# Score products of all attentions: the key's low part in a tile per head, 128 rows in both passes

## The chip, the cores and the metric

The kernel runs on one core of one Trainium2 chip. The metric is device time in microseconds (us), the median of several executions of the same program.

## What is computed

The reference is a network of four layers over 512 tokens and 1024 features, in float32. What matters here are its attentions: three kinds in the first two layers (a retention, a selected attention behind an indexer, a dilated attention), one in the third.

```
def hybrid_layer(x, ...):                    # twice
    proj = rms_norm(x, attn_norm_w) @ w_in
    ...                                      # retention 4 heads, selected attention 4, dilated 8, 64 features each
    x = x + mixed @ w_out
    return x + square(relu(rms_norm(x) @ w_up)) @ w_down
...
    logits = einsum('bqhd,bsd->bqhs', qib, k_idx)          # indexer: 8 query heads, one key
    inner = einsum('bhncd,bhnmd->bhncm', qc, kc) * decay   # retention
    s = einsum('bqhd,bshd->bhqs', qb, k) * scale           # the other attentions, then softmax, then @ v
```

Block 2 follows with an attention of 8 heads with forget gates (the "even" mixer), a gated linear recurrence (the "odd" mixer), and a gated feed-forward after each.

## The kernel before

Activations lie feature-major, [128 features, 512 tokens] per tile. A float32 operand is split into two float32r parts, high and low (`split`), and a product of two operands takes three passes on TensorE: high by high, high by low, low by high (`mm3`, lines 319 to 321). Weights are loaded by SyncE's queue, ScalarE makes the high part (line 266), VectorE or GpSimd the low part (line 267, tiles `whi`, `wlo`).

A score product (keys against queries of one head) has only 64 features to contract over, half of the 128 rows of the array. `head_product` (lines 305 and 306) makes it in two passes. In the first, one operand (`stacked`) has the high part of the head on 64 partitions and its low part on the other 64, and the other operand (`doubled`) has the high part twice, so that 128 rows give high by high and low by high at once. In the second pass, the 64 partitions of the high part meet the low part of the other operand: both operands are cut to `own`, the head's 64 partitions. `doubled` makes the low parts of a pair of heads as one tile `lo`, head 0 on partitions 0 to 63 and head 1 on 64 to 127 (line 297, on VectorE or GpSimd). The phase keeps two such tiles.

There are 208 score products: in each of the first two layers 24 of the indexer, 16 of the retention, 32 of the dilated attention and 16 of the selected one; in the third layer 32. `attend` issues the four products of a head (widths 128, 256, 384, 512), VectorE reduces each (line 521), ScalarE takes the exponential, VectorE and GpSimd scale (line 528), TensorE transposes (line 539), and `weighted_values` multiplies by the values (lines 488 and 490; the second with 64 columns of weights). Between heads, `fill()` lets other projections follow. The indexer's key exists once for all heads, already on all 128 partitions in two copies, high and low.

Each engine works through its own instructions in order. Their order comes from a scheduler that places each instruction by its own estimate when the program is built; a tile's buffer that is used again makes the new writer wait for the old readers. A background job on VectorE (`top_keys`, lines 643 and 644) takes the largest 128 scores step by step between the products.

Before the first weights arrive, `keep_warm(14)` issues 14 products on a zero bfloat16 tile that nothing reads.

Of the kernel before, what the change touches and what calls it, by code (L numbers as in the profile page):

```python
# [8 lines left out]
F = mybir.dt.float32  # L9
R = mybir.dt.float32r  # L10
# [5 lines left out]
S = 512  # L16
# [144 lines left out]
class Net:  # L161
    def __init__(self, ctx, tc, I, out):
# [22 lines left out]
        self.keep_warm(14)  # L185
# [28 lines left out]
    @contextmanager  # L214
    def phase(self, **bufs):
        """The tiles of one phase; the next phase's take their place."""
        with self.tc.tile_pool(name=self.name("phase"), bufs=1, reuse_waits="tile") as pool:
            self.pool, self.bufs = pool, bufs
            yield
# [4 lines left out]
    def act(self):  # L224
        """The two parts of a [128, 512] operand."""
        t = self.get("act", 2 * S, R)
        return t[:, :S], t[:, S:]
# [49 lines left out]
    def stacked(self, t, low=None):  # L277
        """The two parts of each of the two heads of t, one above the other: [high | low] of the first head and
        [low | high] of the second along the partitions."""
# [8 lines left out]
    def doubled(self, t, low=None):  # L288
        """The operand to go with stacked(): the high part of each of the two heads of t, twice along the
        partitions, and the low parts."""  # L290
        nc = self.nc
        ab, lo = self.act(), self.get("lo", S, R)
        for h, s in enumerate(ab):
            own, other = slice(64 * h, 64 * h + 64), slice(64 - 64 * h, 128 - 64 * h)
            nc.scalar.activation(s[own], t[own], AF.Copy)
            nc.scalar.activation(s[other], t[own], AF.Copy)
            (low or nc.vector).tensor_sub(lo[own], t[own], s[own].bitcast(F))
        return ab, lo

    def head_product(self, ps, hh, stacked, rows, doubled, cols, last=True):  # L300
        """ps = a.T @ b for head hh, a and b given by stacked() and doubled()."""
        mm = self.nc.tensor.matmul
        own = slice(64 * hh, 64 * hh + 64)
        a, (b, lo) = stacked[hh], doubled
        mm(ps, a[:, rows], b[hh][:, cols], start=True, stop=False, skip_group_check=True)  # L305
        self.last_mm = mm(ps, a[own, rows], lo[own, cols], start=False, stop=last, skip_group_check=True)  # L306

    def split_scaled(self, x, g, to=None):
        """x * g (per partition) into two parts."""
# [6 lines left out]
    def mm3(self, ps, w, a, first, last):  # L316
        """ps += w.T @ a for operands (high, low)."""
# [5 lines left out]
    def fm_tile(self, w, acts, off=0):  # L323
        """One 128-feature tile: [128 features, 512 tokens]."""
        return self.fm_tiles([(w, off)], acts)[0]

    def fm_tiles(self, ws, acts):
        """Several 128-feature tiles, all of them taking each chunk of acts as it comes, until the last two."""
# [14 lines left out]
    def catch_up(self):  # L343
        """What was put off until after some products."""
# [4 lines left out]
    def tm_half(self, ps, h, src, acts, width, low=None):  # L349
        """Half of the contraction of a token-major product; ps: a [128 tokens, width] psum for each block of  # L350
        128 tokens, made by the first half."""
# [16 lines left out]
    def tick(self):  # L368
        """Lets one step of the work in the background follow."""
# [3 lines left out]
    def after(self, inst, other):  # L373
        """Keeps inst from being issued ahead of other."""
# [3 lines left out]
    def not_before(self, inst):  # L378
        """Keeps work of the background from being issued ahead of the products it is to run beside."""
# [9 lines left out]
    def sumsq(self, chunks, g=None, acc=None, apart=False, eng=None):  # L389
        """The sum over chunks of their squares, each scaled by g(c) per partition; the last one apart, where  # L390
        the time to add it would show."""
# [15 lines left out]
    def mean_sq(self, accs, dim, eps=EPS, warm=False):  # L407
        """accs: [128, tokens] tiles, summed over partitions and tiles; the mean per token plus eps, token-major
        [128, 4]."""
# [13 lines left out]
    def keep_warm(self, n, after=None):  # L423
        """Products that nothing reads, for the tensor engine's clock to stay up while it waits."""
        ps = self.st_tile()
        for _ in range(n):
            mm = self.nc.tensor.matmul(ps, self.identb, self.identb.unsqueeze(1).to_broadcast([128, 4, 128]),
# [9 lines left out]
    def spread_psum(self, r):  # L437
        """r ([128 tokens, 4]) along the free axis, the same on all partitions: by three bfloat16 parts, which
        together are r."""
# [15 lines left out]
    def spread(self, r):  # L455
        """As spread_psum, in SBUF and after the products that follow first."""
# [9 lines left out]
    def values(self, n):  # L466
        """n tiles for the values of four heads, token-major, each head as [high | low]."""
# [5 lines left out]
    def put_values(self, v, tb, ps, r):  # L473
        """ps ([128 tokens, 4 heads x 64]) scaled by r [128,1] and split."""
# [6 lines left out]
    def weighted_values(self, o, hh, pt, v):  # L481
        """The rows of o for head hh: its values.T @ pt, over the causal blocks. The product of both parts of the
        values with the high part of pt takes one pass, low by high coming out below high by high."""
# [12 lines left out]
    def attend(self, pairs, fill):  # L496
        """Softmax attention of pairs of heads. Each of pairs gives, when its turn comes, q (already times
        -1/8) and k (feature-major), the values, mask(qb), added to the negated scores, an operand pair for
        a further term of these (or None) and what to do with the result [2 heads x 64, 512].
        fill() lets other products follow, for the tensor engine to do meanwhile."""  # L500
# [472 lines left out]
    def even_mixer(self):  # L973
# [41 lines left out]
        v = va  # L1015
# [271 lines left out]
```

## Time and profile before

| | |
|---|---|
| runs | 2552.95, 2553.09, 2555.98 us; median 2553.09 |
| profiled execution | span 2550.8 us from the first to the last instruction; the median lies 2.3 us above |
| TensorE matmul | 2482.1 us busy, 97% of the span, 11217 instructions |
| VectorE | 1361.0 us, 53% |
| ScalarE | 1042.9 us, 41% |
| GpSimd | 596.9 us, 23% |
| granted TensorE clock | 0.985 of full speed on average |

Matmul records overlap, since the ends of pipelined matmuls are modelled: the time that one takes from the next is read from start to start, not from its duration. The shares are averages over stages that have different limits. L305 is line 305 of the kernel before.

### The profile page before, as it was taken

Reading aid. Unit: us, or ns where it says so; the run is one execution under the profiler, and the core shown is the slowest. Engines: PE = TensorE matmul, PEld = TensorE weight load, DVE = VectorE, ACT = ScalarE, POOL = GpSimd, SP = SyncE. Lnnn points to the kernel's source line nnn. Section 1 sums busy time; section 2 is a strip of 40 time slices with the busy share of each in tenths; the row PEclk is TensorE's granted clock in tenths of the full one; section 3 lists DMA queues with packets and bytes.
Section 4 is the critical chain, followed back from the end, with each engine's and each line's share of the span. In section 5 each row is a group of like instructions: output and inputs, shape, how many; then the busy total and the mean of one; then the engine's idle time right before and its main releaser. Section 6 shows DMA issues by size and latency. Waiting matters only on the chain.

```text
span 2550.8 us, 28988 instructions
## 1 busy us (share of the span) xinstructions
PE 2482.1 (97%) x11217; PEld 1968.7 (77%) x11217; DVE 1361.0 (53%) x2216; ACT 1042.9 (41%) x1625; POOL 596.9 (23%) x395
## 2 busy tenths in 40 slices
PE   9999999999998999999999999999999989999997
PEld 6687788888876877888888777788887767788886
DVE  6968653333468686433336857533335865533434
ACT  5556552332355665422333464322223564322222
POOL 2355410110033643200111342110101453110101
PEclk9999999999998999999999999999999999999998
DMA  4311123222222111322222211222222222222221
GB/s 144 108 59 46 58 91 99 92 97 94 92 85 89 55 45 62 106 93 95 95 92 86 75 59 50 91 93 97 91 93 81 75 83 75 91 93 97 91 93 64
DMA packets 61514, 215.30 MB, mean 84 GB/s; under 512 B 6849, under 2 KB 6977, under 8 KB 61377
## 3 DMA queue, kind: packets, MB, share of 16 engines
q1 hardware_dynamic: 59760, 207.06, 24.6%
q0 software_dynamic: 1472, 6.29, 0.8%
q8 instruction: 88, 1.44, 0.2%
q14 instruction: 50, 0.40, 0.1%
q10 hardware_dynamic: 144, 0.11, 0.0%
HBM read 211.33 MB, written 2.10 MB: 84 GB/s over the span
## 4 chain that ended last, share of the span: by engine, by line
PE 85%; DVE 10%; issue 2%; ACT 2%; POOL 1%; DMA 0%; SPq 0%; DVEq 0%; ACTq 0%; POOLq 0%
PE mm L321 25%; PE mm L320 25%; PE mm L319 25%; PE st L306 3%; PE st L305 2%; DVE x L943 1%; PE st L539 1%; PE av L488 1%; PE av L490 1%; ACT xg L312 1%; PE av L414 1%; DVE hs L1169 1%; DVE xg L313 1%; DVE score L644 1%; DVE act L285 1%
## 5 line engine op out<-in xcount | busy, mean ns | idle before, releaser
L266 ACT ACTIVATE whi<-raw 128x1024 fp32r<-128x1024 f32 (+3 forms) x398 | 409.8, 1032 | 1156.8 <-PE mm L320 967.2
L319 PE MATMUL mm<-xg,whi 128*128 128x512 f32 x1792 | 704.0, 397 | 14.3 <-ACT xg L312 12.3
L321 PE MATMUL mm<-xg,wlo 128*128 128x512 f32 x1792 | 715.1, 399 | 2.1 <-DVE wlo L267 2.1
L320 PE MATMUL mm<-xg,whi 128*128 128x512 f32 x1792 | 714.2, 399 | 0.2
L319 PE MATMUL mm<-act,whi 128*128 128x512 f32 x1160 | 456.2, 396 | 10.2 <-ACT act L273 8.3
L321 PE MATMUL mm<-act,wlo 128*128 128x512 f32 x1160 | 461.9, 398 | 0.0
L320 PE MATMUL mm<-act,whi 128*128 128x512 f32 x1160 | 460.4, 397 | 1.4 <-POOL act L274 1.4
L267 DVE TENSOR_TENSOR wlo<-raw,whi 128x1024 fp32r<-128x1024 f32 (+2 forms) x289 | 348.5, 1207 | 136.3 <-ACT whi L266 135.5
L319 PEld LDWEIGHTS mm<-xg,whi 128*128 128x128 f32 x1792 | 340.9, 191 | 103.8 <-ACT xg L312 20.8
L274 POOL TENSOR_TENSOR act<-t,act 128x512 fp32r<-128x512 f32 x108 | 150.4, 1394 | 1106.0 <-ACT act L273 1073.3
L320 PEld LDWEIGHTS mm<-xg,whi 128*128 128x128 f32 x1792 | 338.4, 189 | 84.7 <-DVE xg L313 6.6
L321 PEld LDWEIGHTS mm<-xg,wlo 128*128 128x128 f32 x1792 | 338.0, 189 | 79.4 <-DVE wlo L267 4.5
L267 POOL TENSOR_TENSOR wlo<-raw,whi 128x1024 fp32r<-128x1024 f32 (+3 forms) x109 | 257.2, 2362 | 335.9 <-ACT whi L266 312.9
L319 PEld LDWEIGHTS mm<-act,whi 128*128 128x128 f32 x1160 | 221.4, 191 | 62.5 <-ACT act L273 9.7
L320 PEld LDWEIGHTS mm<-act,whi 128*128 128x128 f32 x1160 | 218.8, 189 | 53.7 <-POOL act L274 2.3
L321 PEld LDWEIGHTS mm<-act,wlo 128*128 128x128 f32 x1160 | 218.6, 188 | 47.5
L871 DVE TENSOR_TENSOR x<-x,mm 128x512 f32<-128x512 f32 x64 | 44.0, 688 | 206.2 <-PE mm L321 206.2
L863 DVE SCALAR_TENSOR_TENSOR t<-mm,rb 128x512 f32<-128x512 f32 x64 | 44.1, 691 | 198.8 <-PE mm L321 198.6
L1234 DVE TENSOR_TENSOR t<-mm,rb 128x512 f32<-128x512 f32 x44 | 30.4, 691 | 141.5 <-PE mm L321 141.5
L1232 DVE TENSOR_TENSOR t<-mm,rb 128x512 f32<-128x512 f32 x44 | 30.4, 691 | 118.1 <-PE mm L321 118.1
L273 ACT ACTIVATE act<-t 128x512 fp32r<-128x512 f32 x114 | 72.2, 633 | 49.2 <-DVE t L1235 32.9
L305 PE MATMUL st<-act,act 128*128 128x128 f32 (+3 forms) x208 | 77.5, 373 | 12.5 <-DVE act L285 7.8
(222 smaller groups left out, 2650.4 us busy)
## 6 DMA issues: line engine op xcount, KB each, us to landing
raw<-in_w1up SPq DMA_DIRECT2D x64, 512.0 KB, 3.3
raw<-in_w1down SPq DMA_DIRECT2D x64, 512.0 KB, 3.3
raw<-in_gate SPq DMA_DIRECT2D x44, 512.0 KB, 3.3
raw<-in_up SPq DMA_DIRECT2D x44, 512.0 KB, 3.3
raw<-in_w1fm SPq DMA_DIRECT2D x41, 512.0 KB, 3.3
raw<-in_down SPq DMA_DIRECT2D x32, 512.0 KB, 3.3
raw<-in_odin SPq DMA_DIRECT2D x16, 512.0 KB, 3.3
raw<-in_w1out SPq DMA_DIRECT2D x16, 384.0 KB, 3.0
```

Of the source, the lines that this page charges most:

```text
L266: nc.scalar.activation(hi[:, sl], raw[:, sl], AF.Copy)
L267: (low or nc.gpsimd).tensor_sub(lo[:, sl], raw[:, sl], hi[:, sl].bitcast(F))
L273: nc.scalar.activation(hi, t, AF.Copy)
L274: (low or nc.vector).tensor_sub(lo, t, hi.bitcast(F))
L305: mm(ps, a[:, rows], b[hh][:, cols], start=True, stop=False, skip_group_check=True)
L306: self.last_mm = mm(ps, a[own, rows], lo[own, cols], start=False, stop=last, skip_group_check=True)
L319: mm(ps, w[0], a[0], start=first, stop=False, skip_group_check=True)
L320: mm(ps, w[0], a[1], start=False, stop=False, skip_group_check=True)
L321: self.last_mm = mm(ps, w[1], a[0], start=False, stop=last, skip_group_check=True)
L863: nc.vector.scalar_tensor_tensor(t, ps, 0.0, rb, op0=OP.max, op1=OP.mult)
L871: nc.vector.tensor_add(x[j], x[j], ps)
L1232: nc.vector.tensor_mul(t, pg, rb)
```

## The change

`doubled` now makes a `lo` tile per head. GpSimd sets the other head's 64 partitions to zero, and the subtraction writes the own ones. `head_product` drops the cut to `own`: its second pass takes all 128 rows of the first pass's stationary operand and all 128 of `lo`, with zeros where the low part of the stationary operand stands. The phases keep four `lo` tiles in place of two, so a buffer still comes back after two pairs. For the indexer nothing is written to memory in addition: its low part already lies on all partitions, and its second pass now multiplies low by low as well. The first 14 products that keep the clock up take a zero float32r tile in place of the bfloat16 one, and the memory for descriptors of GpSimd's own transfers is set to 8192. Comments are gone too, and lines move by 1 to 3.

```
+        zero = self.cp.tile([128, 128], R, name="zero")
+        nc.vector.memset(zero.bitcast(F), 0.0)
-        self.keep_warm(14)
+        self.keep_warm(14, of=zero)
...
     def doubled(self, t, low=None):
-        ab, lo = self.act(), self.get("lo", S, R)
+        ab, lo = self.act(), [self.get("lo", S, R) for _ in range(2)]
         for h, s in enumerate(ab):
             own, other = slice(64 * h, 64 * h + 64), slice(64 - 64 * h, 128 - 64 * h)
+            nc.gpsimd.memset(lo[h][other].bitcast(F), 0.0)
             nc.scalar.activation(s[own], t[own], AF.Copy)
             nc.scalar.activation(s[other], t[own], AF.Copy)
-            (low or nc.vector).tensor_sub(lo[own], t[own], s[own].bitcast(F))
+            (low or nc.vector).tensor_sub(lo[h][own], t[own], s[own].bitcast(F))
         return ab, lo
 
     def head_product(self, ps, hh, stacked, rows, doubled, cols, last=True):
         mm = self.nc.tensor.matmul
-        own = slice(64 * hh, 64 * hh + 64)
         a, (b, lo) = stacked[hh], doubled
         mm(ps, a[:, rows], b[hh][:, cols], start=True, stop=False, skip_group_check=True)
-        self.last_mm = mm(ps, a[own, rows], lo[own, cols], start=False, stop=last, skip_group_check=True)
+        self.last_mm = mm(ps, a[:, rows], lo[hh][:, cols], start=False, stop=last, skip_group_check=True)
...
-        with self.phase(act=10, lo=2, v=2, o=1, pr=2, ph=2, pl=2, score=1, gt=2):
+        with self.phase(act=10, lo=4, v=2, o=1, pr=2, ph=2, pl=2, score=1, gt=2):
...
-                    self.head_product(ps[:, :n], hh, q, qs, ((ki[0], ki[0]), ki[1]), slice(0, n))
+                    self.head_product(ps[:, :n], hh, q, qs, ((ki[0], ki[0]), (ki[1], ki[1])), slice(0, n))
...
-        with self.phase(act=6, lo=2, v=2, o=1, pr=2, ph=2, pl=2, m=8, sg=1, row=2):
+        with self.phase(act=6, lo=4, v=2, o=1, pr=2, ph=2, pl=2, m=8, sg=1, row=2):
...
-    nc = _bacc.Bacc("TRN2", target_bir_lowering=False, num_devices=1)
+    nc = _bacc.Bacc("TRN2", target_bir_lowering=False, num_devices=1, dynamic_dma_scratch_size=8192)
```

TensorE's order stays as it was, line for line, but for the last heads of the first two layers, where the scheduler mixes passes of two heads and a projection a little differently. GpSimd's order gets 40 new instructions, 16 in each of the first two layers and 8 in the third. In the dilated attention of the first layer, GpSimd's instructions were these (`wlo` are low parts of weights, `pr` the softmax rows of a head that are being scaled, `act` a stacked operand):

```order
46 L267 TENSOR_TENSOR wlo_1864<-raw_1861,whi_1863 128x1024
47 L528 TENSOR_SCALAR pr_1647<-pr_1647,rc_1650 128x128
48 L528 TENSOR_SCALAR pr_1647<-pr_1647,rc_1650 128x256
49 L267 TENSOR_TENSOR wlo_1935<-raw_1932,whi_1934 128x1024
50 L267 TENSOR_TENSOR wlo_2023<-raw_2020,whi_2022 128x1024
```

At the same place the order is now this:

```order
58 L269 TENSOR_TENSOR wlo_1878<-raw_1875,whi_1877 128x1024
59 L297 MEMSET lo_2080 64x512
60 L531 TENSOR_SCALAR pr_1661<-pr_1661,rc_1664 128x128
61 L531 TENSOR_SCALAR pr_1661<-pr_1661,rc_1664 128x256
62 L269 TENSOR_TENSOR wlo_1952<-raw_1949,whi_1951 128x1024
63 L269 TENSOR_TENSOR wlo_2040<-raw_2037,whi_2039 128x1024
```

A MEMSET of the last dilated pair's low tile has come between the low part of weights and the scaling of a head's rows; it waits for the last score product of the third dilated head (head 0 of the second pair), whose tile had that buffer.

At the start of the second layer GpSimd's order was this (`act` belongs to the feed-forward before, `rstd` to the norm of the new layer):

```order
120 L274 TENSOR_TENSOR act_5151<-t_5148,act_5151 128x512
121 L434 TENSOR_TENSOR rstd_5468<-var_5466,mhalf 128x4
122 L267 TENSOR_TENSOR wlo_5669<-raw_5666,whi_5668 128x1056
```

Now it is this:

```order
140 L276 TENSOR_TENSOR act_5177<-t_5174,act_5177 128x512
141 L297 MEMSET lo_6082 64x512
142 L297 MEMSET lo_6083 64x512
143 L297 MEMSET lo_6221 64x512
144 L297 MEMSET lo_6222 64x512
145 L437 TENSOR_TENSOR rstd_5494<-var_5492,mhalf 128x4
146 L269 TENSOR_TENSOR wlo_5695<-raw_5692,whi_5694 128x1056
```

Four MEMSETs, which wait for tiles of the feed-forward in the same memory to come free, now stand ahead of the norm's `rstd`.

## Rows read from the trace of the kernel before

**Rows 1.** The page: busy time, share of the span and instructions of each engine.

```profile
PE 2482.1 (97%) x11217; PEld 1968.7 (77%) x11217; DVE 1361.0 (53%) x2216; ACT 1042.9 (41%) x1625; POOL 596.9 (23%) x395
```

**Rows 2.** The chain that ended last, shares of the span by line.

```profile
by line: PE mm L321 25.4%; PE mm L320 25.4%; PE mm L319 25.2%; PE st L306 2.7%; issue 2.0%; PE st L305 1.9%; DVE x L943 1.3%; PE st L539 1.0%; PE av L488 0.9%; PE av L490 0.8%; ACT xg L312 0.7%; PE av L414 0.6%; DVE hs L1169 0.6%; DVE xg L3
```

**Rows 3.** Instructions of line 306, forms kept apart; durations in ns, rows*columns of the array.

```profile
L306 PE MATMUL st<-lo,act x160: 322/435/792, 93.7 to 1545.1; 64*128 64x512 f32 x40, 64*128 64x384 f32 x40, 64*128 64x128 f32 x40, 64*128 64x256 f32 x40
```

**Rows 4.** Timeline of all engines around 60 us: start us, us, engine, line.

```profile
59.13 0.39 PE L319 MATMUL mm<-xg,whi 128*128 128x512 f32 x1
59.13 0.19 PEld L320 LDWEIGHTS mm<-xg,whi 128*128 128x128 f32 x1
...
60.02 0.69 DVE L587 TENSOR_TENSOR t<-mm,rb 128x512 f32<-128x512 f32 x1 [2.04 <-PE mm L321]
60.02 0.18 PEld L306 LDWEIGHTS st<-act,act 64*128 64x128 f32 x1 [0.24 <-issue]
60.02 0.38 PE L306 MATMUL st<-act,act 64*128 64x256 f32 x1
...
60.34 0.44 PE L305 MATMUL st<-act,act 128*128 128x384 f32 x1
```

**Rows 5.** Timeline of TensorE's matmuls, one dilated head and the values' products behind it.

```profile
179.52 0.22 PE L305 MATMUL st<-act,act 128*128 128x128 f32 x1
...
181.72 0.49 PE L306 MATMUL st<-lo,act 64*128 64x512 f32 x1
182.15 0.50 PE L488 MATMUL av<-ph,v 128*128 128x512 f32 x1
182.48 0.39 PE L490 MATMUL av<-pl,v 128*64 128x512 f32 x1
182.71 0.34 PE L488 MATMUL av<-ph,v 128*128 128x384 f32 x1
182.89 0.34 PE L490 MATMUL av<-pl,v 128*64 128x384 f32 x1
183.06 0.28 PE L488 MATMUL av<-ph,v 128*128 128x256 f32 x1
...
183.30 0.22 PE L488 MATMUL av<-ph,v 128*128 128x128 f32 x1
183.36 0.23 PE L490 MATMUL av<-pl,v 128*64 128x128 f32 x1
```

**Rows 6.** Windows: length, busy us of PE, PEld, DVE, ACT, POOL; clock; DMA.

```profile
60.00:80.00 20.00, 20.00 (x73) 13.12 (x73) 19.36 (x37) 11.25 (x21) 9.45 (x7) 1.00 0.32 104
80.00:100.00 20.00, 17.87 (x64) 13.14 (x63) 19.75 (x37) 15.03 (x22) 8.63 (x5) 0.86 0.26 91
200.00:220.00 20.00, 20.00 (x92) 15.60 (x92) 16.71 (x46) 12.17 (x24) 15.24 (x12) 1.00 0.19 60
240.00:260.00 20.00, 17.61 (x87) 13.15 (x85) 16.57 (x32) 16.11 (x34) 6.04 (x5) 1.00 0.12 35
1480.00:1500.00 20.00, 20.00 (x93) 15.31 (x94) 9.33 (x24) 9.71 (x20) 8.09 (x5) 1.00 0.20 63
```

**Rows 7.** Timeline of TensorE: two indexer products, and the retention's first product.

```profile
40.00 0.38 PE L306 MATMUL st<-act,act 64*128 64x256 f32 x1
...
55.36 0.49 PE L306 MATMUL st<-act,act 64*128 64x512 f32 x1
...
93.26 0.51 PE L305 MATMUL st<-act,act 128*128 128x512 f32 x1 [2.13 <-DVE act L285]
```

**Rows 8.** Timeline of GpSimd: a low part of weights, and its one large MEMSET.

```profile
180.96 2.38 POOL L267 TENSOR_TENSOR wlo<-raw,whi 128x1024 fp32r<-128x1024 f32 x1 [1.91 <-issue]
...
1386.22 0.53 POOL L1046 MEMSET sg<- 128x512 f32 x1 [5.28 <-PE av L414]
```

**Rows 9.** Timeline of TensorE at the start.

```profile
0.98 5.44 PE L427 MATMUL st<-identb 128*128 128x512 bf16 x14 [0.98 <-DVE mhalf L197]
7.04 0.50 PE L319 MATMUL mm<-xg,whi 128*128 128x512 f32 x1 [0.61 <-ACT whi L266]
```

More of the change, by code (lines that the diff above doesn't have):

```diff
@@ L421, in mean_sq, with keep_warm @@
         return var
-    def keep_warm(self, n, after=None):
+    def keep_warm(self, n, after=None, of=None):
         ps = self.st_tile()
         for _ in range(n):
-            mm = self.nc.tensor.matmul(ps, self.identb, self.identb.unsqueeze(1).to_broadcast([128, 4, 128]),
+            t = self.identb if of is None else of
+            mm = self.nc.tensor.matmul(ps, t, t.unsqueeze(1).to_broadcast([128, 4, 128]),
                                        start=True, stop=True, skip_group_check=True)
```

## The prediction

> **What bounds the kernel now.** I first read the busy times of the page: TensorE's matmuls cover 97% of the span, the next engine 53% [rows 1]. The span is 2550.8 us, and what an engine other than TensorE costs can only show where TensorE waits for it. Then the chain of waits, by line: three quarters of it are the projections' passes (L319 to L321), which the change doesn't touch; the score products have 2.7% (L306) and 1.9% (L305), together 4.6% or 117 us of 2550.8 [rows 2]. So I looked at what a score product costs. There are 160 outside the indexer [rows 3] and its 2 x 24 = 48, together 208, and the reader should look not at durations but at starts. In one dilated head the four products (widths 128, 256, 384, 512, two passes each) run from 179.52 to 182.15, 2.63 us [rows 5]. The values' products behind them have the same widths and all 128 rows, the second of each pair with 64 columns: 512 wide takes 0.23 us to the next start (182.48 to 182.71), 384 wide 0.18 (182.71 to 182.89), 256 wide 0.12 (half of 183.06 to 183.30), 128 wide 0.06 (183.30 to 183.36) [rows 5]. At these prices two passes of four widths would be 2 x 0.59 = 1.18 us, not 2.63.
>
> Why: in the projections the next weights are loaded from the moment the present matmul starts (both at 59.13). The weights of a 64-row pass start to load only together with that pass (both at 60.02), after the sequencer has stood with no named wait for 0.24 us; and the 128-row pass after it comes 0.32 us later (60.34) for 256 columns, which cost 0.12 elsewhere [rows 4]. The toll is paid going into 64 rows, in them, and once more behind: L488 at 182.15 takes 0.33 to the next start, its like 0.23 [rows 5].
>
> **The change, part by part.** *The cut to 64 rows goes.* Toll per head: 2.63 - 1.18 + 0.10 behind = 1.55 us, or 0.39 per product. If a 128-wide pass with its own weights took 0.11 in place of 0.06, it would be 0.36. I take 0.38. 208 x 0.38 = 79 us of TensorE's time is the upper bound of the gain; the bounds of the price give 75 to 81. The second pass streams as many columns as before, and the 64-column passes right there show that a matmul next to unlike neighbours need not pay (0.18 and 0.12 us, like their 128-column partners) [rows 5].
>
> The page "TensorEngine Tiling (Array Packing)" of the Trainium skill (Key Properties) says that changing the tiling mode, not just the tile, drains the engine. For 64 rows the trace agrees (0.39 us a product); for 64 columns it doesn't (0.12 us for 256 columns on either side). By the rule alone the 160 column passes would pay too, and the sum for this change would be the same 79 us.
>
> *What of it reaches the end.* Stage by stage, for each of the first two layers:
> - Indexer, 24 products. Twelve of them lie between 40.00 and 55.36 [rows 7]; VectorE then waits 2.04 us for a projection at 60.02 [rows 4], so these 12 x 0.38 = 4.5 us bring it forward. From there VectorE is full (19.36 and 19.75 of 20 us), and TensorE waits for it 2.13 us at 93.26 [rows 6, 7]. The other twelve only lengthen that wait: 4.5 of 9 us.
> - Retention, 16 products, 6 us. Two groups of four lie where TensorE has just waited for VectorE and is next on the chain, and part of a third; two others are covered by VectorE. I count 5, with a little more for those at half clock (0.86 in 80 to 100, [rows 6]).
> - Dilated heads 0 to 5, 24 products, 9 us: TensorE is full and VectorE has 16.71 of 20 us in the busiest part [rows 6], so there is slack for it: 9.
> - Dilated heads 6 and 7, 8 products, 3 us: TensorE is busy 17.61 of 20 us and VectorE and ScalarE hold 16.57 and 16.11 in their turn [rows 6]: 1.5.
> - Selected attention, 16 products, 6 us: short waits on VectorE and ScalarE alternate with TensorE: 4.5.
>
> That is 24.5 us a layer, 49 for two. In the third layer's 32 products TensorE is full while VectorE has 9.33 and ScalarE 9.71 of 20 us [rows 6]: 11.5 of 12. Sum 60.5 us. It fits the chain: 117 us of it are score passes, of which 0.38 in each 0.66 us (2.63 / 4) is toll, 67 us, before anything else becomes late.
>
> *GpSimd's 40 MEMSETs.* The one like them, 128x512, took 0.53 us [rows 8]; 64 partitions with the same 512 columns I take as 0.5, at most 0.53, at least nothing on the path: 20 us on an engine that is 23% busy [rows 1]. They stand behind weights' low parts and ahead of the scaling of softmax rows. A MEMSET waits for the last reader of a buffer two pairs old. For the place shown: the work before it ends at 180.96 + 2.38 = 183.34 [rows 8], the reader is done by 182.15 [rows 5], so it doesn't wait and only delays the head's scaling by 0.5 us, which TensorE's projections between the scores and the transposes cover. Without that cover all 40 would cost 20 us. I charge 3.
>
> *Longer idle stretches of TensorE* at 93 and its like, after which the clock has been low before (0.86, [rows 6]): between nothing and 4 us; I charge 1.5. *The four MEMSETs ahead of `rstd`* take 2 us while the norm's squares are summed: nothing, 2 us for each of two layers if uncovered. *The start:* the 14 products end 0.61 us before the first real one, which waits for ScalarE [rows 9]; in float32r they may be as quick or take up to a microsecond more; nothing. *The descriptors' memory:* twelve transfers, none on the chain; nothing.
>
> Sum: 60.5 - 4.5 = 56 us. The profiled execution's 2550.8 becomes 2495; with the 2.3 us between it and the median of the runs, 2497.
>
> **Rivals.**
> 1. *Nearly all of the toll comes back:* VectorE's stretches move together with TensorE, and the products covered at 60 to 90 shorten later waits. For it: TensorE's 97%. Against: VectorE at 19.75 of 20. 2553 - 79 = 2474; I call everything below 2483 this.
> 2. *VectorE takes it:* only the third layer and dilated heads 0 to 5 pay out, 32 + 2 x 24 = 80 products, 30 us, with the MEMSETs off the path: 2523; everything above 2513 this. For it: VectorE's order is fixed and the background job sits between the reductions. Against: three quarters of the chain are TensorE's projections [rows 2], which VectorE merely follows.
> 3. *No gain:* the loss belongs to the second pass as such (a wait for `lo`), not to its 64 rows: 2553. Against: the indexer's `lo` was ready long before, and its products pay the same (0.32 for 256 columns, [rows 4]).
>  The page "TensorE: Matmul & The Clock Gate" of the Trainium skill (Part 3, what overlaps) says that weights load beside running matmuls only when they go to other rows of the array. By that rule 128-row passes would load alone, and the change would give nothing, 2553. The trace disagrees: 128-row weights at 59.13 load beside a 128-row matmul [rows 4].
> 4. *Slower:* MEMSETs hold GpSimd until TensorE has passed a head, with `wlo` queued behind them, so that TensorE waits for weights. 30 of the 40 stand alone or first in a group and wait for an old reader. It decides from 56 / 30 = 1.9 us each on the path; at 3 us each it gives 2497 + 90 = 2587. Against: at the place shown the reader is done 1.2 us before GpSimd arrives (182.15, 183.34), and TensorE will be earlier than that by some more.
>
> **How the numbers follow.** My case, 2483 to 2513 around 2497: 55%. Rival 1: 19%. Rival 2: 20%. Rival 3: 3%. Rival 4: 3%. The range must leave out no more than 2 in 10; 2471 to 2524 takes in rival 1 and most of rival 2, and leaves the rest. 0.2% of 2553 is 5 us, about what runs of this kernel can tell from no change. Faster by more than that: 55 + 19 + 20 = 94%; within: 3%; slower: 3%.
>
> **What the profile after would show.** If right: the passes of the second line of `head_product` have 128*128, a head's four products take 1.2 to 1.3 us in place of 2.63, and 128-row weights load beside the matmul before. TensorE's busy time falls by some 75 us and its idle time grows by some 20. The wait of the retention's first product for VectorE at 93.26 grows to 5 to 7 us. The third layer's mixer ends 11 to 12 us sooner relative to its start, each of the first two some 22 us. Wrong would be: products that still take 0.3 us for 256 columns (rival 3); new waits of TensorE for `wlo` from GpSimd with a MEMSET ahead (rival 4); or idle time that grows by 50 us and waits for VectorE (rival 2).

## The result, and the profile after

The changed kernel takes 2497.17 us (median of 4 runs, 2494.83 to 2504.59) against 2554.53 for the kernel before beside it; the ratio is 0.978, 95% interval 0.9763 to 0.9797. That is 57 us less, and the forecast was 2497. But the sum that led there had two wrong terms that nearly cancelled, the toll (too high) and the clock (wrong in sign), as the experiments and the accounting behind them show. The profiled execution has a span of 2493.0 us (before 2550.8), and its mean granted clock is 0.992 (before 0.985).

The busy line of the page after, to be read against [rows 1]:

```profile
PE 2404.7 (96%) x11217; PEld 1950.8 (78%) x11217; DVE 1360.7 (55%) x2217; ACT 1039.4 (42%) x1625; POOL 619.0 (25%) x435
```

TensorE has the same 11217 matmuls and is busy 77.4 us less; VectorE and ScalarE are as busy as before. So TensorE's idle time (span less busy) grew by 19.6, from 68.7 to 88.3 us. GpSimd's 40 new instructions are 22 us of busy time.

The chain by line, against [rows 2] (every line number is up by 2 in `head_product` and `mm3`):

```profile
by line: PE mm L323 24.4%; PE mm L322 24.4%; PE mm L321 24.1%; issue 2.7%; DVE x L946 1.3%; DVE score L647 1.1%; PE st L307 1.1%; DVE m L646 1.0%; PE st L308 0.8%; PE st L542 0.8%; DVE m L1143 0.8%; ACT xg L314 0.7%; DVE act L287 0.7%; PE a
```

The score products have gone from 4.6% of the chain to 1.9%, 117 us to 47. VectorE's background job (L646 and L647, 2.1% or 52 us) is now among the costliest lines of the chain; in [rows 2] neither of its lines stands above 0.6%.

The timeline of TensorE for the same dilated head as in [rows 5]:

```profile
165.34 0.22 PE L307 MATMUL st<-act,act 128*128 128x128 f32 x1
165.40 0.27 PE L308 MATMUL st<-lo,act 128*128 128x128 f32 x1
165.51 0.33 PE L307 MATMUL st<-act,act 128*128 128x256 f32 x1
...
166.40 0.39 PE L308 MATMUL st<-lo,act 128*128 128x512 f32 x1
166.63 0.39 PE L491 MATMUL av<-ph,v 128*128 128x512 f32 x1
166.86 0.39 PE L493 MATMUL av<-pl,v 128*64 128x512 f32 x1
```

Four products take 1.29 us (165.34 to 166.63) in place of 2.63. The first values' product takes 0.23 to the next start, no longer 0.33. The passes with 64 columns, L493, still cost nothing extra. A 128-wide pass with weights of its own takes 0.11 (165.40 to 165.51).

The timeline around an indexer product, matmuls and weight loads, where [rows 4] shows the loads of before:

```profile
55.20 0.19 PEld L307 LDWEIGHTS st<-act,act 128*128 128x128 f32 x1
55.43 0.28 PE L307 MATMUL st<-act,act 128*128 128x256 f32 x1
55.44 0.19 PEld L308 LDWEIGHTS st<-act,act 128*128 128x128 f32 x1
55.55 0.28 PE L308 MATMUL st<-act,act 128*128 128x256 f32 x1
55.55 0.19 PEld L307 LDWEIGHTS st<-act,act 128*128 128x128 f32 x1
```

The second pass's weights load from 55.44, beside the first pass that began at 55.43, and 256 columns take 0.11 to 0.12 us. By the rule of the Trainium skill's page "TensorE: Matmul & The Clock Gate" (Part 3, what overlaps) that stood beside rival 3, taken by itself, weights for the same rows would load alone; the trace of the changed kernel disagrees as that of before did.

What TensorE waits for, by what it waits on (total us, times, longest us), after:

```profile
PE st L307 <- DVE act L287: 8.8, 6, 2.3
...
PE st L719 <- DVE t L713: 6.3, 3, 3.4
PE st L307 <- DVE pl L547: 5.4, 5, 1.3
PE av L491 <- ACT ph L546: 4.5, 7, 1.2
PE st L307 <- DVE mn L524: 4.2, 4, 1.5
PE av L491 <- DVE o L497: 4.0, 3, 1.9
```

The same view of the kernel before has these:

```profile
PE st L305 <- DVE act L285: 7.8, 4, 2.1
PE st L305 <- DVE pl L544: 4.7, 4, 1.3
...
PE av L488 <- DVE o L494: 0.9, 2, 0.5
PE st L716 <- DVE t L710: 0.6, 3, 0.2
PE av L488 <- ACT ph L543: 0.6, 3, 0.2
```

All named waits of TensorE sum to 55.5 us before and 74.4 after. What grew is not one wait but several short ones, most of them at places where TensorE hardly waited before: the group norm behind the retention (L719), the transposed rows (`ph`), the tile a score product needs next (`mn`), the sum of the values (`o`).

Windows of after, for the stretches of [rows 6] that they answer to (20 us each; the work in them has moved forward by up to 17 us, so they hold roughly the same work):

```profile
60.00:80.00 20.00, 19.14 (x82) 15.15 (x83) 19.89 (x43) 13.16 (x22) 8.97 (x6) 1.00 0.40 138
80.00:100.00 20.00, 17.67 (x84) 14.39 (x83) 19.82 (x40) 15.26 (x23) 9.63 (x7) 1.00 0.34 110
180.00:200.00 20.00, 18.44 (x94) 15.21 (x93) 17.37 (x46) 13.56 (x27) 15.74 (x11) 1.00 0.15 55
220.00:240.00 20.00, 17.50 (x105) 14.24 (x103) 17.44 (x38) 16.68 (x34) 5.72 (x6) 1.00 0.07 21
```

From 60 to 100 VectorE stays full. In the dilated heads TensorE, which was full in the first of the two windows (20.00) and had 17.61 in the second, now has 18.44 and 17.50; VectorE is not full either, with 17.4 of 20 us in both.

### The profile page after: what moved, and what is told of

It reads as the page before. It is cut to its first block, busy times and chain, and to the rows that moved or that the text cites. A ratio compares the mean times of both kernels' runs of the same rounds, so it can differ in the third digit from the quotient of the medians.

```text
span 2493.0 us, 29049 instructions
## 1 busy us (share of the span) xinstructions
PE 2404.7 (96%) x11217; PEld 1950.8 (78%) x11217; DVE 1360.7 (55%) x2217; ACT 1039.4 (42%) x1625; POOL 619.0 (25%) x435
## 4 chain that ended last, share of the span: by engine, by line
PE 78%; DVE 14%; ACT 4%; issue 3%; POOL 1%; DMA 0%; ACTq 0%; DVEq 0%; POOLq 0%
PE mm L323 24%; PE mm L322 24%; PE mm L321 24%; DVE x L946 1%; DVE score L647 1%; PE st L307 1%; DVE m L646 1%; PE st L308 1%; PE st L542 1%; DVE m L1143 1%; ACT xg L314 1%; DVE act L287 1%; PE av L416 1%; DVE hs L1172 1%; PE av L491 1%
## 5 line engine op out<-in xcount | busy, mean ns | idle before, releaser
L321 PE MATMUL mm<-xg,whi 128*128 128x512 f32 x1792 | 699.1, 394 | 14.3 <-ACT xg L314 12.1
L1237 DVE TENSOR_TENSOR t<-mm,rb 128x512 f32<-128x512 f32 x44 | 30.4, 691 | 141.8 <-PE mm L323 141.8
L1235 DVE TENSOR_TENSOR t<-mm,rb 128x512 f32<-128x512 f32 x44 | 30.4, 691 | 118.1 <-PE mm L323 118.1
L307 PE MATMUL st<-act,act 128*128 128x128 f32 (+3 forms) x208 | 72.2, 356 | 20.8 <-DVE act L287 8.8
```

Source lines behind the costliest of these rows:

```text
L321: mm(ps, w[0], a[0], start=first, stop=False, skip_group_check=True)
L1235: nc.vector.tensor_mul(t, pg, rb)
L1237: nc.vector.tensor_mul(u, pu, rb)
```

## The experiments

The theories on trial (other letters stand for rivals that the expectations describe where they come up): **A**, the toll belongs to the 64-row passes and is paid where the array changes between 128 and 64 rows; **D**, other parts of the change (MEMSETs, four low tiles, the new start) matter; **E**, what did not arrive was taken by VectorE's load.

**Experiment 1: the indexer alone.** The kernel before, with 128 rows in the indexer's second pass only. No MEMSET is needed there.

```
-        own = slice(64 * hh, 64 * hh + 64)
+        own = slice(64 * hh, 64 * hh + 64) if own is None else own
...
-                    self.head_product(ps[:, :n], hh, q, qs, ((ki[0], ki[0]), ki[1]), slice(0, n))
+                    self.head_product(ps[:, :n], hh, q, qs, ((ki[0], ki[0]), ki[1]), slice(0, n),
+                                      own=slice(0, 128))
```

> The kernel before, with 128 rows in the second pass of the indexer's 48 products alone; no MEMSET, no new tile. Theory A (a toll of 0.38 us for each product with 64 rows, of which VectorE takes back part): the indexer's products lose their toll, 24 x 0.38 = 9 us of TensorE a layer, and 4.5 to 6.5 us of it reach the end, so 9 to 13 us less in all, 0.995 to 0.996 of before. Rival B (the second pass waits for its low part, whatever its rows): the indexer's low part is ready long before, so nothing changes, 1.000. Rival C (VectorE takes all of the indexer's gain): the 64-column and 128-row starts show no toll, but the time is within 0.1% of before.

Measured: 2542.47 us, ratio 0.9946 (0.9927 to 0.9966), some 14 us by the ratio, 10.5 by the spans (2550.8 to 2540.3). That is theory A's time, but not its working: the toll of these 48 products was not 18 us but some 14 (below), and most of it, not half, reached the end.

**Experiment 2: everything but the indexer.** The changed kernel, the indexer's second pass cut to 64 rows again.

```
-                    self.head_product(ps[:, :n], hh, q, qs, ((ki[0], ki[0]), (ki[1], ki[1])), slice(0, n))
+                    self.head_product(ps[:, :n], hh, q, qs, ((ki[0], ki[0]), (ki[1], ki[1])), slice(0, n),
+                                      own=slice(64 * hh, 64 * hh + 64))
```

> The changed kernel, with the indexer's second pass back at 64 rows. Theory A: it keeps the other 160 products' gain, 2497 + 9 to 13 = about 2508, 0.981 to 0.984 of before. Rival C (the indexer's part is worth nothing because VectorE is full right behind it): 0.978, as the whole change. If the parts do not add (each opens the way for the other), it is above 0.984.

Measured: 2515.36 us, ratio 0.9833 (0.9807 to 0.9859). 0.54% of the first experiment and 1.67% of this one make 2.21%; the whole change gives 2.2%. Within their intervals the parts add.

**Experiment 3: all but the rows.** The changed kernel, MEMSETs, four tiles and new start included, with every second pass cut to the head's 64 partitions.

```
+        own = slice(64 * hh, 64 * hh + 64)
-        self.last_mm = mm(ps, a[:, rows], lo[hh][:, cols], start=False, stop=last, skip_group_check=True)
+        self.last_mm = mm(ps, a[own, rows], lo[hh][own, cols], start=False, stop=last, skip_group_check=True)
```

> The changed kernel with all its MEMSETs, four tiles and the new start, but every second pass cut to 64 rows as before. Theory A: the toll stays, and the MEMSETs cost 0 to 4 us, 1.000 to 1.0015 of before. Rival D (each MEMSET of 0.5 us delays something that TensorE waits for): 40 x 0.5 = 20 us more, 1.008.

Measured: 2553.44 us, ratio 0.9996 (0.9983 to 1.0008). The busy line of its page:

```profile
PE 2482.3 (97%) x11217; PEld 1971.1 (77%) x11217; DVE 1362.5 (53%) x2217; ACT 1043.0 (41%) x1625; POOL 618.8 (24%) x435
```

GpSimd has its 22 us more, TensorE is as busy as before (2482.1, [rows 1]), and the time is the same. The whole gain comes from the 128 rows, and the 40 MEMSETs cost nothing: D falls. The form's line in the changed kernel (busy us, mean ns, then idle time ahead and what ended it):

```profile
L297 POOL MEMSET lo<- 64x512 f32 x40 | 21.5, 539 | 63.9 <-PE mm L323 37.9 <-PE st L308 24.6 <-POOLq L1282 0.3
```

They do wait for readers, 24.6 us for score products in all; that this delays nothing that reaches the end is what experiment 3's unchanged time shows, there with 64 rows.

**Experiment 4: zeros written once.** The four low tiles of a phase are taken once and used in turn, so that 12 MEMSETs do in place of 40.

```
+    def zeroed(self):
+        self.los, self.turn = [self.get("lo", S, R) for _ in range(4)], 0
+        for i, t in enumerate(self.los):
+            h = i % 2
+            self.nc.gpsimd.memset(t[64 - 64 * h:128 - 64 * h].bitcast(F), 0.0)
...
-        ab, lo = self.act(), [self.get("lo", S, R) for _ in range(2)]
+        ab, lo = self.act(), [self.los[2 * self.turn + h] for h in range(2)]
+        self.turn = 1 - self.turn
...
-            nc.gpsimd.memset(lo[h][other].bitcast(F), 0.0)
```

> The changed kernel, but the zeros are written once per phase into four tiles that are kept (head 0 and head 1 always come back to their own tile), 12 MEMSETs in place of 40. Theory A: 0 to 4 us less than the change, 0.9765 to 0.978 of before. Rival D: 28 x 0.5 = 14 us less, 0.9725.

Measured: 2504.76 us, ratio 0.9799 (0.9775 to 0.9823), above both theories' numbers; the interval just takes in theory A's upper end, but all four executions (2503.1 to 2511.1) lie above the forecast 2497. The third layer's mixer takes 197.2 us in place of 185.0. The waits of TensorE there have a line that the changed kernel has not:

```profile
PE st L314 <- DVE lo L306: 5.8, 1, 5.8
```

The first score product of the third layer waits for its own low part. The edit gave the scheduler other dependences and VectorE got that subtraction later; that this is the whole of the 12 us was not tried on its own.

**Experiment 5: the 64-row pass twice.** The kernel before issues each second pass a second time, so the low part counts twice in the scores.

```
+        mm(ps, a[own, rows], lo[own, cols], start=False, stop=False, skip_group_check=True)
         self.last_mm = mm(ps, a[own, rows], lo[own, cols], start=False, stop=last, skip_group_check=True)
```

> The kernel before with its 64-row pass issued twice in a row, so that the low part is added twice (the scores change by that). It tells where the toll is paid. Theory A1 (each 64-row pass pays, whatever stands before it): between the two 64-row passes the start-to-start time is as it was between a 64-row and a 128-row pass, about 0.31 us for 256 columns and 0.42 for 512, and a head's four products take 2.6 + 1.4 = 4.0 us. Theory A2 (only the change between 64 and 128 rows pays): the first of the two 64-row passes takes the plain 0.12 and 0.23 us to the second, and a head takes 2.6 + 0.6 = 3.2 us.

Measured: one execution, 2602.78 us, 48 more than before (span 2600.9, clock 0.980). Timeline of TensorE's passes and weight loads, where L306 and L307 are the two equal passes:

```profile
182.01 0.38 PE L305 MATMUL st<-act,act 128*128 128x256 f32 x1
182.32 0.18 PEld L306 LDWEIGHTS st<-lo,act 64*128 64x128 f32 x1
182.32 0.38 PE L306 MATMUL st<-lo,act 64*128 64x256 f32 x1
182.43 0.19 PEld L307 LDWEIGHTS st<-lo,act 64*128 64x128 f32 x1
182.55 0.28 PE L307 MATMUL st<-lo,act 64*128 64x256 f32 x1
182.75 0.19 PEld L305 LDWEIGHTS st<-act,act 128*128 128x128 f32 x1
182.75 0.44 PE L305 MATMUL st<-act,act 128*128 128x384 f32 x1
```

The three passes have the same 256 columns and take 0.31 (into 64 rows), 0.23 (from 64 rows to 64 rows) and 0.20 us (out of them); the 128-row passes of the changed kernel took 0.11 to 0.12 in the timeline at 55.43. From L305 to the next L305 it is 0.74 us. Over all 256-wide products the second pass took 0.31 us when it stood alone and 0.22 and 0.21 when doubled: the extra pass costs 0.12, the price of a plain pass. The other widths agree (0.11, 0.18 and 0.23 to 0.24 for 128, 384 and 512 columns). So the toll is not the pass's own: theory A2's sum came (a head of four products takes 3.25 to 3.28 us, forecast 3.2), though not its row, since the first of the two passes did not fall to 0.12 alone. The weight loads show where the toll sits. Weights for other rows than the pass before begin to load only together with their own pass (182.32 into 64 rows, 182.75 out of them); those of the second 64-row pass begin at 182.43, 0.12 ahead of it. The 48 us are 34 for the 208 extra passes (the medians of each width) and some 14 for half clock (44 us in place of 30, counted as in the table below).

**Experiment 6: the 128-row pass twice.** The same doubling in the changed kernel.

```
+        mm(ps, a[:, rows], lo[hh][:, cols], start=False, stop=False, skip_group_check=True)
         self.last_mm = mm(ps, a[:, rows], lo[hh][:, cols], start=False, stop=last, skip_group_check=True)
```

> The changed kernel with its second pass issued twice in a row (low part added twice). Both theories: each pass takes the plain 0.12 us for 256 and 0.23 us for 512 columns, a head's four products about 1.9 us in place of 1.3, and the time is at most 208 x 0.15 = 31 us above the changed kernel, 2505 to 2528. If plain passes were only so quick because there are two of them, it shows here as more.

Measured: one execution, 2524.87 us, 28 more than the change's median (30 by the spans, 2523.0 and 2493.0). In its trace the 208 extra passes cost 34 us at the medians of each width (0.11, 0.12, 0.18 and 0.23 us), not the 31 of the forecast. So most of the added work is paid; with one execution, and those of the change between 2494.83 and 2504.59, the share is between some 20 and 30 of 34 us.

**Experiments 7 and 8: half of the top keys.** The kernel before and the changed one, each with 8 steps of the background job in place of 16; half of the key selection is left out. VectorE has 42 us less to do.

```
-            for _ in range(16):
+            for _ in range(8):
```

> The kernel before with 8 in place of 16 steps of the indexer's background job on VectorE (so only 64 keys are marked). It takes some 24 us of VectorE's work out of each of the first two layers. Theory A (VectorE holds the time in parts of these layers): 5 to 15 us less than before. To be read with the next run.

> The changed kernel with 8 in place of 16 steps of the background job on VectorE. Theory A (the rest of the toll, 79 - 57 = 22 us, is taken by VectorE in the first two layers): the change is worth more with VectorE lighter, 65 to 75 us between this run and the one before it, so 0.965 of before or less. Rival E (the toll was only 57 us, or is lost to latency between the engines and not to VectorE's load): the difference stays at 55 to 60 us.

Measured: 2547.97 us, ratio 0.9963 (0.9951 to 0.9974), and 2489.47 us, ratio 0.9737 (0.9718 to 0.9757). Between them lie 58.5 us; with the full job it was 57. E falls as the explanation of the total. At one place it holds. First products of dilated heads 4, 5 and 6 in the changed kernel:

```profile
195.01 0.22 PE L307 MATMUL st<-act,act 128*128 128x128 f32 x1
211.84 0.22 PE L307 MATMUL st<-act,act 128*128 128x128 f32 x1
227.12 0.33 PE L307 MATMUL st<-act,act 128*128 128x128 f32 x1 [1.32 <-DVE pl L547]
```

and with half of the keys:

```profile
199.47 0.22 PE L307 MATMUL st<-act,act 128*128 128x128 f32 x1
214.39 0.22 PE L307 MATMUL st<-act,act 128*128 128x128 f32 x1
229.00 0.33 PE L307 MATMUL st<-act,act 128*128 128x128 f32 x1 [0.78 <-DVE pl L547]
```

Head 4 takes 16.83 us with the full job (16.2 before the change) and 14.92 with half. The waits of TensorE in the kernel with half of the keys:

```profile
PE st L719 <- DVE t L713: 10.0, 3, 4.5
PE st L307 <- DVE act L287: 8.9, 6, 2.4
...
PE av L491 <- ACT ph L546: 4.2, 7, 1.0
PE av L491 <- DVE o L497: 4.1, 3, 1.9
```

From the first product of head 4 to that of head 7 the change gains nothing with the full job (47.71 and 47.72 us) and 3.1 us with half of it (45.88 and 42.78). But only the wait for `mn` is gone from the list and the one for `pl` about halved (2.9 us); the waits at the group norm, for `act`, `ph` and `o` are about as long as with the full job or longer. Those stand in chains of small steps on several engines, in which TensorE now arrives early; that it is the chains, and not VectorE's queue, is argued from this and was not tried.

**Experiment 9: zeros once, in the first two layers only.** As experiment 4, the third layer as in the change.

```
+            self.zeroed()
             self.mixers(l)
+            self.los = None
...
+            if self.los is None:
+                nc.gpsimd.memset(lo[h][other].bitcast(F), 0.0)
```

> The changed kernel with the four low tiles of the first two layers taken once per phase and their zeros written once (4 MEMSETs in place of 16 in each layer); the third layer keeps a MEMSET per tile, as in the change. Earlier, with zeros written once in all three layers, the first two were 0.8 and 2.2 us shorter than with the change, and the third 12 us longer, where TensorE waited 5.8 us for a low part that had been put later in VectorE's order. Theory A (the third layer's order was the whole loss, the first two gain a little): 2497 - 3 = 2494 us, ratio 0.976 to 0.978, and a third mixer of 185. Rival B (fewer MEMSETs gain nothing and the 3 us were spread): 2497. Rival C (the third layer's order also shifts here): 2505, with a third mixer of 197.

Measured: 2495.47 us, ratio 0.9762 (0.9746 to 0.9777), third mixer 185.1 us. The change beside it is at 0.9768 (experiment 11): no difference that can be told. Rival B, fewer MEMSETs gain nothing, is the simpler reading, in line with experiment 3; that the third layer's loss came with the edit there, and not from the first two layers, is shown.

**Experiment 10: 64 rows, fewer changes.** The kernel before; the products of a head in `attend` go in pairs, both first passes and then both second ones. Rows, columns and passes are the same; the 64-row passes stand in 146 stretches in place of 208.

```
-                self.head_product(ps[:, :n], hh, q, qs, k, slice(0, n), st is None)
+                for part in (0, 1):
+                    for qb, ps in zip((q0, q0 + 1), tiles):
+                        n = (qb + 1) * 128
+                        qs = slice(qb * 128, n)
+                        self.head_product(ps[:, :n], hh, q, qs, k, slice(0, n), st is None, (part,))
```

> The kernel before, 64-row second passes and all, but the four products of a head in the dilated, selected and third layer's attention are issued in pairs: first pass, first pass, second pass, second pass. TensorE's order then has 146 stretches of 64-row passes in place of 208; passes, rows and columns are the same, with no MEMSET. Theory A (the toll of 0.38 us is paid where the array goes from 128 to 64 rows and back): 62 x 0.38 = 24 us less of TensorE's time, of which 0.72 arrives, as with the change (57 of 79): 17 us, 2537, ratio 0.992 to 0.995. Rival B (the toll belongs to each 64-row pass): 2554, ratio 1.000. Rival C (the later reductions of the first score of each pair, which now waits for two more passes, cost more than the toll): above 2554.

Measured: 2541.63 us, ratio 0.9938 (0.9923 to 0.9954), 16 us less, 9 by the spans of the two profiles (2550.8 and 2541.8): theory A's number by the ratio (17), with neither a row nor a pass changed. The slowest of its executions, 2544.0, is below the fastest of before beside it, 2551.9. Timeline of TensorE (x2 is a row of two matmuls, 128 and 256 wide):

```profile
182.93 0.39 PE L306 MATMUL st<-act,act 128*128 128x128 f32 x2
183.25 0.49 PE L308 MATMUL st<-lo,act 64*128 64x128 f32 x2
183.67 0.44 PE L306 MATMUL st<-act,act 128*128 128x384 f32 x1
```

The two products take 0.74 us (median of 20 such pairs 0.744). Before the change the same two took 1.031 (median of 22), in the changed kernel 0.460. Of 0.571 us of toll for two products, 0.284 is left when one stretch does for both: half of the stretches, half of the toll. The Trainium skill's page "TensorEngine Tiling (Array Packing)" (Key Properties), by which a change of tiling mode drains the engine, fits the toll here for 64 rows; for 64 columns the timelines of [rows 5] and of the changed kernel show no such cost.

**Experiment 11: the change once more,** beside the two before.

> The changed kernel once more, unaltered, beside the two others on the same chip, so that differences of 2 or 3 us can be read. All theories: 2497, ratio 0.976 to 0.980.

Measured: 2497.29 us, ratio 0.9768 (0.9753 to 0.9783); span 2496.7, clock 0.990.

## Why the prediction was right, and where it was not

To see where the time went I added up, for all 11217 matmuls, the time from each start to the next beyond what its columns take at full clock (about 0.215 us for 512, the price of the kernel's bfloat16 products; one profiled execution of each kernel), and put it down to one of three: what lies beside a second pass of a score product; half of the time in stretches at half clock (1.2 in place of 2.4 GHz) up to the last product; all the rest. The second is the most that the clock can have cost, since waits in these stretches count too. The rest holds the named waits (55.5 and 74.4 us) and, for the larger part, what float32r passes take above 0.215 us (0.23 for 512 columns). The columns' own time is the same in both kernels, some 2148 us.

| us | before | after | difference |
|---|---|---|---|
| beside second passes | 87.4 | 21.8 | -65.6 |
| half clock | 30.4 | 14.0 | -16.4 |
| the rest | 270.8 | 294.5 | +23.7 |
| sum | | | -58.3 (spans: -57.8) |

For experiment 11 the differences are -65.8, -12.1 and +23.4.

- **The mechanism: right, shown.** Going to 64 rows and back costs time on TensorE. Experiment 3 has everything of the change but the rows and gains nothing; experiment 10 has fewer changes of rows, with the same passes in another order, and gains 16 us; experiment 5 shows that a second pass on the same rows adds only the price of a plain pass, its weights loading ahead. The traces agree at every place: in the kernel before, wherever the rows change (206 times into 64 rows and 206 out of them, long waits left out), the weights begin to load together with their pass, within 0.01 us; between two 128-row passes they begin 0.23 us ahead (median), and between two 64-row passes 0.17 in experiment 5 and 0.06 in experiment 10. What keeps the weights back, a drain of the array or another cause, no run tells apart.
- **The toll's size, 0.38 us x 208 = 79: too large.** 65.6 / 208 is 0.32, below the lower bound of 75. The price came from one head of four products in a row with what lies behind it; with the 0.11 us for a 128-wide pass, which the prediction named and took only in part, that head gives 0.36, as measured ((2.63 - 1.29 + 0.10) / 4). Other patterns are cheaper: 0.29 a product in the 128 and 256 wide pairs of experiment 10's comparison, and by the same sum some 0.29 in the indexer (13.7 us for 48, experiment 1). One pattern's price was carried to all. The prediction's own check by the chain, 67 us, was nearer to it.
- **The clock, charged as a loss of up to 4 us: wrong in sign.** It gave at most 12 to 16 us by the table; counting only the columns of passes that began in such stretches, the doubling is 23.2 us before, 11.2 after and 13.9 in experiment 11, a gain of 9 to 12. In the profiled executions the granted clock is 0.985 to 0.987 in the kernels with the 64-row passes as they were or in pairs (before, experiments 3, 7, 10), and 0.990 to 0.992 in all with 128 rows throughout (the change twice, experiments 4, 6, 8, 9); over all executions the two groups meet, with 0.982 to 0.989 and 0.987 to 0.993. In the first layer before, half clock began at 94.3, 121.6, 142.1 and 261.6 us, 20.4 us in all; in the profile after it began once, at 127.3, for 6.8 us, during the wait of 3.38 us that ended at 128.44, and in experiment 11 twice, at 88.1 and 129.1, for 10.2 us. The prediction took longer waits to mean more half clock; most of these stretches went, although TensorE waited 2.33 us at 86.93, 2.13 before ([rows 7]). Why they went is open. The window at the last of the four (length, busy us of PE, PEld, DVE, ACT, POOL, clock, DMA), before:

```profile
260.00:280.00 20.00, 19.94 (x80) 13.76 (x79) 14.12 (x40) 10.47 (x29) 4.18 (x5) 0.83 0.08 26
```

and after, there and around 127.3:

```profile
127.00:135.00 8.00, 6.56 (x34) 6.57 (x35) 6.49 (x12) 3.28 (x6) 3.13 (x4) 0.57 0.19 68
260.00:280.00 20.00, 19.64 (x99) 15.69 (x98) 14.71 (x39) 12.97 (x31) 12.76 (x10) 1.00 0.28 93
```

- **TensorE's busy time -75, idle time +20: both came as forecast** (-77.4 and +19.6), but the first is two terms, 66 of toll and the rest of clock. That it fitted was luck, and the total was right for the same reason.
- **What reaches the end, stage by stage.** From start to start of the norms' products, the first two layers' mixers became 24.1 (24.7 from the start of the span) and 23.1 us shorter (forecast 24.5 each, some 22 with the charges), the third's 9.1 (forecast 11.5). Inside the first: indexer and retention 12.1 up to the first dilated product (forecast 9.5); dilated heads 0 to 5 about 5 (forecast 9); head 6 nothing; head 7 and the selected attention 7.6 (forecast for heads 6, 7 and selected together 6), of which up to 3.4 is the half-clock stretch at 261.6 that is gone. Rival 2's reason, that VectorE takes the gain, held for dilated heads 4 to 6, as experiments 7 and 8 show (3.1 us there with half of the job, nothing with the full one), although it counted heads 4 and 5 among those that pay; for the layer it was wrong, since the whole difference stayed at 58.5 us: what a lighter VectorE gave there was lost again elsewhere.
- **The wait at 93.26 would grow to 5 to 7 us: wrong.** It is 2.33 us at 86.93. The step that failed is "from there VectorE is full", so that twelve of the indexer's products would only lengthen that wait. VectorE is full there (19.89 and 19.82 of 20), but the retention's first product came 6.3 us sooner, not 4.5. In the first 60 us VectorE got 40.4 us of work done in place of 36.6: it had been waiting there, and its work, made of the indexer's products, started earlier when these did.
- **MEMSETs, 3 us: nothing** (experiment 3). Rival 4 falls with that. The part about `wlo` queued behind them was argued from one place; among the waits of TensorE after there is none for a `wlo` of GpSimd.
- **Rivals 1 and 3.** 2474 would have needed waits that shorten; the named ones grew by 19 us, the rest of the table by 24. Rival 3 falls by experiments 3 and 10.

The largest single new wait, at the group norm, as the timeline of the changed kernel shows it:

```profile
123.53 1.98 POOL L712 TENSOR_TENSOR rs<-vr,mhalf 128x8 f32<-128x8 f32 x1 [1.20 <-DVE vr L711]
125.50 2.33 POOL L269 TENSOR_TENSOR wlo<-raw,whi 128x1024 fp32r<-128x1024 f32 x1
125.55 2.83 DVE L713 TENSOR_TENSOR t<-t,rs 128x512 f32<-128x512 f32 x1 [1.57 <-POOL rs L712]
128.44 0.90 PE L719 MATMUL st<-const_sb,t 128*128 128x128 f32 x3 [3.38 <-DVE t L713]
```

GpSimd's 1.98 us for eight columns, then VectorE's 2.83 us for 512 while GpSimd makes a `wlo` beside it, and TensorE stands 3.38 us. Before, this norm cost TensorE 0.2 us at most. The same two instructions in the kernel before:

```profile
138.69 0.69 DVE L710 TENSOR_TENSOR t<-t,rs 128x512 f32<-128x512 f32 x1 [1.57 <-POOL rs L709]
138.97 2.62 POOL L267 TENSOR_TENSOR wlo<-raw,whi 128x1024 fp32r<-128x1024 f32 x1 [0.31 <-ACT whi L266]
```

There VectorE's multiplication began first and took 0.69 us; now the `wlo` begins 0.05 us ahead of it, and it ends 0.5 us behind the `wlo`. The second layer shows the same pair of times (0.69 and 2.83 us), and so does experiment 11. So some 2.1 of the 3.38 us go with GpSimd's `wlo` coming first, and not with the chain's own length. Another order of the two was not tried.

## What to carry to other kernels

Read the price of a matmul from start to start, beside neighbours of the same and of another shape: a pass on 64 rows between passes on 128 paid about 0.3 us here that its columns don't explain, and filling up the rows with zeros takes it away, while putting 64-row passes next to each other pays it once for all of them. Before multiplying such a price, take it in each pattern in which the instruction stands, not in the dearest. When TensorE gets shorter, expect short waits to open in the norm and softmax chains (here named waits grew by 19 us against 66 saved), look at what now runs beside each step of such a chain, and count the stretches at half clock as a term of either sign.

## What the runs showed that I had not expected

- **Fewer 64-row passes went with less time at half clock**: 30.4 us for half clock before, 14.0 and 18.3 in two executions of the change; the kernel with each 64-row pass doubled has the lowest clock of all, 0.980. Experiment 10, with as many 64-row passes in fewer stretches, did not have less (some 32).
- **Added work on TensorE cost most of its price** (28 of 34 us for a doubled 128-row pass, one execution), **while work removed** returned 42 of 66 us before the clock's part. Whether the two shares differ, one execution can't tell.
- **The same VectorE instruction took 0.69 or 2.83 us**, by whether GpSimd's `wlo` began behind it or ahead of it.
- **64 columns are free where 64 rows are not**: 166.86 to 167.09, 0.23 us for 512 columns, as for 128 columns beside it.
